# A two-layer attention and Mamba-2 kernel: the second x tile is transposed into the scan's PSUM buffers, and the second layer's start writes its decay tables with six stores

## The chip, the cores and the metric

The kernel runs on one core of a Trainium2 chip, as a single launch. The metric is the device time of one execution in microseconds. The engines are called as the profile calls them: PE (TensorE, matmuls and transposes) with its weight loads PEld, DVE (VectorE), ACT (ScalarE), POOL (GpSimd) and SP (SyncE, which here issues DMAs). "SPq" in a row of the profile is a DMA issue on SP.

## The reference

A latent stream of 1024 tokens by 1024 features goes through two layers: gated windowed attention, then a gated bidirectional Mamba-2 (SSD) mixer. Each is wrapped in an adaLN-modulated RMS norm and a gated residual. 256 context tokens supply keys and values to the attention, and initial states to the scans. The change lies wholly in the second layer:

```python
def front(h):                        # for the latents and for the context
    z, xbc, dt_raw = split(h @ w_in)
    xbc = silu(centred_depthwise_conv(xbc, conv_w, conv_b))      # 5 taps
    xs, bm, cm = split(xbc)          # xs: 8 groups x 256, bm and cm: 8 groups x 128
    dt = softplus(dt_raw + dt_bias)
...
a_cs = cumsum(dt * A, axis=chunk)    # chunks of 128 tokens, both directions
states = einsum(bm, exp(a_last - a_cs), x * dt)
h[c + 1] = exp(a_last[c]) * h[c] + states[c]
y = (cm @ bm.T * exp(a_cs[q] - a_cs[s])) @ (x * dt) + cm @ h[c] * exp(a_cs) + d_skip * x
...
y_lat = (rms_normalize_per_group(y * silu(z)) * norm_w) @ w_out
```

There are 8 groups of 4 heads with 64 columns each, 8 chunks of latents, 2 chunks of context, and everything is kept in float32. A product of matrices is made of three matmuls on a high and a low part of each operand (high by high, low by high, high by low).

## The kernel before, in words

**The groups.** The second layer works through the 8 groups one after the other. `front(g)` makes the inputs of one group: four tiles of 128 features in the order `bT` (keys), the first x tile (kind 0), the second x tile (kind 1), `cT` (queries), and then `z`. For each of the first three tiles a context part (24 matmuls of 128x256 into the PSUM buffer `psD`) comes ahead of the latent part (48 matmuls of 128x512, L1095, into a two-bank buffer `raw` of tag `pj2`); `cT` has the latent part only. `z` then takes 192 matmuls of 128x256 (L1129) into two more buffers of tag `pj2`. PSUM has two buffers `pj2` (two banks each), one `psD` and three `psX` (one bank each). The third tile's `raw` and the first buffer of `z` are therefore the same memory: between them `cT` has taken the other one.

**After the matmuls of a tile**, a queue of steps `post` works it off: an ACT bias step that empties `raw` into `acc`, four convolution taps on DVE (L1011, which still read `raw`), a tanh on ACT back into `raw` (L1018), and a DVE product (L1019) that makes the silu. For `bT` and the two x tiles, `natural` then turns the tile so that tokens lie on the partitions: PE transposes of `acc` into the used `raw` (L1058), four per step, and an ACT copy out of it (L1061) per four. The order of steps in this kernel is transposes, copy, transposes, copy. `z` may start writing when the third tile's last copy has read the buffer.

**The queue.** Each matmul that `front` issues advances the queue's clock by its cost; every POST = 0.5 us of cost pops one step. Steps posted with a delay (LATE = 3.0) wait in a second list until the clock has advanced that far. What the queue gives is the program's order; a list scheduler in the framework then simulates the whole program and reorders the instructions of every engine by readiness, so PE's order is known only from the built program.

**The scan.** While `front(g + 1)` runs, `slot` scans one chunk of group g at a time, five pieces of front work between its parts. It takes five `psX` buffers in turn: `pcb` (L1247), `po` (L1249, L1250), `S` (L1256), `yd` (L1281) and `pt` of the chunk before (L1312, two transposes into `uT`, which is stored as `uN`). `states` is a chain of 11 jobs (matmul L1198 into `psD`, POOL L1173 and L1178, DVE L1210) that makes the initial states of the next group; it starts when `st[1]` is set, that is when the second x tile is done.

**The start of the layer.** `dt_chain` makes the decays: `decay` stores the cumulated decays to DRAM (`acs_d`), `total` stores the chunk totals (`eal_d`, L951, L952) and loads them back broadcast (`eal`, L953); `rows`, at the end of the chain, loads the first two chunks' decay rows (`M` and `bw`, L1221, 256 KB each). After group 0's front, `offset` (POOL L1226), `merge` (DVE L1230, a predicated copy of `bw` into `M`) and `decays` (ACT L1236, exponentials) prepare the first chunk's decay matrix.

**The end.** The output projection (`ssd_out`, 576 matmuls on L1527 in its first part) runs beside the scan of the last group. It takes its features from the stored `uN` through a load (`oraw`, L1473), an ACT cast (L1485) and a DVE subtraction (L1482). The features of group 7 (k = 14, 15) for the first half of the tokens are first read by matmul 337 of the 576.

Of the kernel before, what the change touches and what calls it, by code (L numbers as in the profile page):

```python
# [17 lines left out]
P = 128  # L18
# [15 lines left out]
R = 4  # L34
HP = 64
# [24 lines left out]
OUT = 4 * 30 * 3 * N512  # L60
POST = 0.5
LATE = 3.0
DTPACE = 1.0
SEGS = (1.5, 2.0, 2.0, 2.2, 2.2)
_STOP = None
# [46 lines left out]
class Kernel:  # L112
# [812 lines left out]
    def dt_chain(self, keep, rows):  # L925

        nc, t, ps, p = self.nc, self.t, self.psA, self.ps_
        n = 640
        nb = n // P
        dt = self.dts  # L930
        w1, w2, w3, ea = [t(p, [P, KT // 2, 256], F32, y).rearrange("p a b -> p (a b)")[:, :n] for y in ("xn4", "sz", "sz", "xn4")]
        tot = t(self.pc, [P, 8], F32, "tot", 2)[:, :nb]
        et = t(self.pc, [P, 8], F32, "tot", 2)[:, :nb]
# [1 line left out]
        v, act = nc.vector, nc.scalar.activation  # L935

        def decay():
            for o in (0, 384):
                for y in range(4):
                    d, s = y // 2, (o // 384) * 512 + 256 * (y % 2)  # L940
                    nc.sync.dma_start(self.acs_d[32 * d : 32 * d + 32, s : s + 256], w3[32 * y : 32 * y + 32, o : o + 256])

        def total():
            v.tensor_copy(tot[:64], blocks(w3)[:64, :, P - 1])
            v.tensor_copy(tot[64:], blocks(w3)[64:, :, 0])
            act(et, tot, AF.Exp)
            for y in range(4):
                d, h = y // 2, y % 2
                row = self.eal_d[0][32 * d : 32 * d + 32]
                for o, c in ((0, 2 * h), (3, 4 + 2 * h)):  # L950
                    nc.sync.dma_start(row[:, c : c + 2], et[32 * y : 32 * y + 32, o : o + 2])  # L951
                nc.sync.dma_start(row[:, 8 + h : 9 + h], et[32 * y : 32 * y + 32, 2:3])  # L952
# [5 lines left out]
        def turn(b):  # L958
# [15 lines left out]
        steps = [  # L974
            lambda: v.scalar_tensor_tensor(w1, in0=dt, scalar=-1.0, in1=dt, op0=ALU.mult, op1=ALU.min),
            lambda: act(w1, w1, AF.Exp),
            lambda: v.tensor_scalar_add(w2, w1, 1.0),
            lambda: v.tensor_scalar_add(w3, w2, -1.0),
            lambda: (act(ea, w2, AF.Ln), v.tensor_sub(w1, w1, w3)),
            lambda: v.reciprocal(w3, w2),  # L980
            lambda: v.tensor_mul(w1, w1, w3),
            lambda: v.tensor_add(w1, w1, ea),
# [3 lines left out]
            lambda: v.tensor_tensor_scan(out=w3[:64], data0=keep[:64], data1=w1[:64], initial=0.0, op0=ALU.mult, op1=ALU.add),  # L986
            lambda: v.tensor_tensor_scan(out=w3[64:, ::-1], data0=keep[64:, ::-1], data1=w1[64:, ::-1], initial=0.0, op0=ALU.mult, op1=ALU.add),
            decay,
            total,
            lambda: v.tensor_sub(blocks(w1), tot.unsqueeze(2).broadcast_to([P, nb, P]), blocks(w3)),  # L990
            lambda: act(w1, w1, AF.Exp),
            lambda: v.tensor_sub(w2, w2, w3),
            lambda: v.tensor_mul(w1, w1, dt),
            lambda: act(ea, w3, AF.Exp),
            rows,
        ]
        return steps + [lambda b=b: turn(b) for b in (2, 0, 4, 3, 1)]

# [16 lines left out]
    def silu(self, raw, acc):  # L1015

        nc = self.nc
        return [lambda: nc.scalar.activation(raw, acc, AF.Tanh),  # L1018
                lambda: nc.vector.scalar_tensor_tensor(acc, in0=raw, scalar=1.0, in1=acc, op0=ALU.add, op1=ALU.mult)]  # L1019

    def front(self, g, st, post, first=None, dt=None):

        nc, t, a = self.nc, self.t, self.a
        ps, p, pf = self.psA, self.ps_, self.pf
# [25 lines left out]
        def wz(q):  # L1050
            return lambda: weights(a["w_z"][g, q], 4, 256)

        def natural(raw, acc, dst, o, n):
            steps = []

            def tr(lo, hi):
                for x in range(lo, hi):
                    nc.tensor.transpose(raw[:, x * P : (x + 1) * P], acc[:, x * P : (x + 1) * P], self.ident)  # L1058

            def ev(d, lo, hi):  # L1060
                nc.scalar.copy(d[:, :, o : o + P], raw[:, lo * P : hi * P].rearrange("p (c n) -> p c n", n=P))  # L1061

            for d, lo, hi in dst:
                steps.append(lambda lo=lo, hi=hi: tr(lo, hi))
                steps.append(lambda d=d, lo=lo, hi=hi: ev(d, lo, hi))
            return [(LATE, steps)]

        tiles = [(16 + g, "bT"), (2 * g, 0), (2 * g + 1, 1), (24 + g, "cT")]
        st["xn"] = [t(p, [P, 4, R * HP], F32, "xn4") for _ in range(2)] + [t(p, [P, NCC, R * HP], F32, "xn2")]
# [6 lines left out]
        for n, (x, kind) in enumerate(tiles):  # L1076
# [4 lines left out]
            if nat:  # L1081
                raw = t(ps, [P, 512], F32, "psD")[:, :CTX]
# [24 lines left out]
                    post.append(lambda: self.dt_tail(draw, post, *dt))  # L1107
            post.extend(self.taps(x, raw, acc, 0, LAT, LAT) + self.silu(raw, acc))
            if nat:
                post.extend(natural(raw, acc, [(st[nat[0]][i], 4 * i, 4 * i + 4) for i in range(2)], nat[1], 8))  # L1110

            def done(kind=kind, acc=acc):
                st[kind] = acc

            post.append((LATE, [done]) if nat else done)
        need(w)
        w0, w = w, loads[-1]()
        post.extend(w["steps"])
# [26 lines left out]
    def ssd(self, c0):  # L1145
# [16 lines left out]
        def hd(d, g):  # L1162
            return slice(32 * d + 4 * g, 32 * d + 4 * g + 4)
# [64 lines left out]
        def merge(M, bw):  # L1228

            nc.vector.copy_predicated(M, self.before.unsqueeze(1).broadcast_to([P, R, P]), bw)  # L1230
# [463 lines left out]
```

## Time and profile before

| what | before |
|---|---|
| median of 3 runs | 1809.46 us (1806.79 to 1813.08) |
| the profiled execution | 1807.02 us, span 1805.3 us |
| granted PE clock, mean | 0.993 |
| PE busy | 1739.6 us, 96% of the span |
| DVE, ACT, POOL busy | 65%, 48%, 44% |
| DMA traffic | 227.61 MB, mean 126 GB/s |

The profiled execution spends 1.7 us outside its span. In a row, "start us, us, engine line op out<-in xcount [idle before <-releaser]", the bracket is idle time of that engine ahead of the instruction and what ended it. PEclk in a table of windows is the clock granted to PE, 1.00 being full. Matmuls are pipelined: the distance from one start to the next, not the duration, is what one of them costs PE.

### The profile page before, as it was taken

How to read it: one execution, taken by the hardware profiler on the slowest of the kernel's cores; microseconds unless marked ns; L12 is line 12 of the kernel's file. 1: busy time of each engine (PE TensorE's matmuls, PEld its weight loads, DVE VectorE, ACT ScalarE, POOL GpSimd, SP SyncE). 2: the span in 40 equal slices, each digit the busy share in tenths (PEclk: the TensorE clock that was granted, in tenths of full speed). 3: DMA queues.
4: the chain of work that ended last, by engine and by line, in shares of the span. 5: the costliest groups of instructions: out<-in, count | busy, mean ns of one | idle time of the engine just before them, and what ended most of it. 6: DMA issues, size and time to landing. Idle time of an engine off the chain costs nothing.

```text
span 1805.3 us, 28983 instructions
## 1 busy us (share of the span) xinstructions
PE 1739.6 (96%) x10319; PEld 1494.7 (83%) x10319; DVE 1181.8 (65%) x2115; ACT 867.1 (48%) x1906; POOL 799.0 (44%) x1068
## 2 busy tenths in 40 slices
PE   6899999999999999999999999999999999999997
PEld 2697788888888887778888898988889898888887
DVE  4634436778877885684776858577684867766734
ACT  3612237777777774452443525344353534544522
POOL 2331127555575545103454544645454464554411
PEclk9999999999999999999999999999999999999999
DMA  9558856444455436222222323222332322656533
GB/s 334 226 144 268 283 177 149 106 100 111 111 153 130 120 102 221 73 53 73 71 77 82 92 62 98 79 71 79 81 93 62 100 73 76 174 169 170 175 101 121
DMA packets 212495, 227.61 MB, mean 126 GB/s; under 512 B 16384, under 2 KB 149632, under 8 KB 212352
## 3 DMA queue, kind: packets, MB, share of 16 engines
q1 hardware_dynamic: 178288, 207.12, 38.0%
q0 software_dynamic: 34064, 18.65, 5.8%
q8 instruction: 81, 1.33, 0.3%
q14 instruction: 62, 0.51, 0.1%
HBM read 190.88 MB, written 35.13 MB: 125 GB/s over the span
## 4 chain that ended last, share of the span: by engine, by line
PE 81%; DVE 9%; ACT 4%; DMA 3%; issue 2%; SPq 1%; POOL 1%; DVEq 0%; ACTq 0%; POOLq 0%
PE pj L1095 17%; PE pj L1129 10%; PE pj L1527 7%; PE pj L246 6%; PE pj L247 6%; PE pj L248 6%; PE psD L1085 4%; PE psX L1281 3%; PE pt L684 3%; PE psD L1198 2%; PE pv L691 2%; PE pv L690 1%; PE S L659 1%; PE S L658 1%; PE psX L1249 1%
## 5 line engine op out<-in xcount | busy, mean ns | idle before, releaser
L246 PE MATMUL pj<-uH,wh 128*128 128x512 f32 (+1 forms) x712 | 257.4, 363 | 9.0 <-ACT uH L470 6.3
L247 PE MATMUL pj<-uL,wh 128*128 128x512 f32 (+1 forms) x712 | 243.3, 342 | 0.5 <-POOL uL L707 0.4
L248 PE MATMUL pj<-uH,wl 128*128 128x512 f32 (+1 forms) x712 | 242.4, 341 | 1.4 <-POOL wl L231 1.4
L1095 PE MATMUL pj<-uH,wl 128*128 128x512 f32 x512 | 172.7, 405 | 0.0
L1095 PE MATMUL pj<-uH,wh 128*128 128x512 f32 x512 | 171.4, 405 | 1.2 <-ACT bn L1061 0.7
L1095 PE MATMUL pj<-uL,wh 128*128 128x512 f32 x512 | 169.2, 402 | 0.0
L246 PEld LDWEIGHTS pj<-uH,wh 128*128 128x128 f32 x712 | 135.6, 191 | 36.2 <-ACT uH L470 7.7
L1129 PE MATMUL pj<-wh,uH 128*128 128x256 f32 x512 | 150.3, 294 | 9.1 <-ACT xn L1061 9.1
L1173 POOL TENSOR_TENSOR xw<-xn,dtdec 128x256 f32<-128x256 f32 x144 | 92.9, 650 | 141.6 <-PE psD L1198 107.1
L1129 PE MATMUL pj<-wh,uL 128*128 128x256 f32 x512 | 152.7, 298 | 0.0
L248 PEld LDWEIGHTS pj<-uH,wl 128*128 128x128 f32 x712 | 135.0, 190 | 18.6 <-POOL wl L231 2.3
L247 PEld LDWEIGHTS pj<-uL,wh 128*128 128x128 f32 x712 | 135.8, 191 | 16.0 <-issue 3.0
L1129 PE MATMUL pj<-wl,uH 128*128 128x256 f32 x512 | 146.7, 287 | 0.0
L689 DVE TENSOR_TENSOR pl<-pt,ph 128x512 fp32r<-128x512 f32 x168 | 114.1, 688 | 47.2 <-ACT ph L688 46.2
L231 POOL TENSOR_TENSOR wl<-wr,wh 128x512 fp32r<-128x512 f32 x76 | 100.2, 1322 | 86.1 <-ACT wh L229 85.2
L663 DVE CUSTOM_DVE_ANT_0 sm<-S,mask,nsink 128x640 f32<-128x640 f32 (+2 forms) x160 | 119.2, 773 | 19.8 <-PE S L659 12.6
L665 ACT ACTIVATE sm<-sm,nm 128x640 f32<-128x640 f32 (+2 forms) x160 | 118.6, 742 | 16.6 <-DVE nm L663 15.9
L688 ACT CAST ph<-pt 128x512 fp32r<-128x512 f32 x168 | 97.5, 586 | 56.0 <-PE pt L684 52.7
L229 ACT CAST wh<-wr 128x512 fp32r<-128x512 f32 (+1 forms) x116 | 74.7, 648 | 87.7 <-PE pj L247 63.5
L1095 PEld LDWEIGHTS pj<-uH,wl 128*128 128x128 f32 x512 | 95.3, 188 | 19.2
L1095 PEld LDWEIGHTS pj<-uL,wh 128*128 128x128 f32 x512 | 95.4, 188 | 18.7
L1129 PEld LDWEIGHTS pj<-wh,uH 128*128 128x128 f32 x512 | 98.7, 193 | 13.5 <-ACT xn L1061 12.1
(339 smaller groups left out, 4810.8 us busy)
## 6 DMA issues: line engine op xcount, KB each, us to landing
wr<-w_x SPq DMA_DIRECT2D x32, 512.0 KB, 4.6
M<-acs SPq DMA_DIRECT2D x64, 256.0 KB, 4.9
bw<-acs SPq DMA_DIRECT2D x64, 256.0 KB, 5.5
wr<-w_sk SPq DMA_DIRECT2D x24, 512.0 KB, 3.8
wr<-wg SPq DMA_DIRECT2D x40, 256.0 KB, 4.5
qs<-q POOLq DMA_DIRECT2D x40, 256.0 KB, 3.9
wada<-w_ada SPq DMA_DIRECT2D x16, 512.0 KB, 7.2
wr<-wq SPq DMA_DIRECT2D x32, 256.0 KB, 3.0
```

Source lines behind the costliest of these rows:

```text
L231: (eng or nc.vector).tensor_tensor(l, raw, h, op=ALU.subtract)
L246: self.nc.tensor.matmul(ps, lh, rh, start=first and i == 0, stop=False)
L247: self.nc.tensor.matmul(ps, lh, rl, start=False, stop=False)
L248: self.last_mm = self.nc.tensor.matmul(ps, ll, rh, start=False, stop=last and i == n - 1)
L663: nc.vector.tensor_tensor_reduce(out=sm[:, :W], in0=Sv, in1=self.mask[:, m0 : m0 + W], scale=-SCALE, scalar=self.nsink[:, 4 * j + r : 4 * ...
L665: nc.scalar.activation(sm[:, :W], sm[:, :W], AF.Exp, bias=nm[:, r : r + 1], scale=-1.0, accum_out=sums[:, r : r + 1])
L688: nc.scalar.copy(ph, ptf)
L689: nc.vector.tensor_sub(pl, ptf, ph)
L1095: nc.tensor.matmul(raw[:, 512 * i : 512 * i + 512], l[:, k, :], r[i][:, k, :], start=k + y == 0, stop=k == KT - 1 and y == 2)
L1129: nc.tensor.matmul(pj[:, c], l, r[:, k, :], start=c % 2 + q + k + y == 0, stop=c % 2 == 1 and q == 1 and k == 3 and y == 2)
L1173: nc.gpsimd.tensor_tensor(xw, X(st, c).rearrange("p (r h) -> p r h", r=R), self.dtdec[:, c, hd(d, g)].unsqueeze(2).broadcast_to([P, R, HP] ...
L1527: nc.tensor.matmul(banks[x], l[:, z, sl], r, start=k == 2 * qs[0] and y == 0, stop=k == 2 * qs[-1] + 1 and y == 2)
```

## The change

**The turnings.** `natural` gets a parameter `apart`, which is set for the latent part of the second x tile. There each set of four transposes goes into a `psX` buffer of its own, and the copies read those; `raw` is no longer used after the silu product. The steps wait LAST = 6.8 instead of 3.0, and `st[1]` is set at the same delay, so that the chain of states starts later. For the other tiles both sets of transposes are one step, still into `raw`, followed by the two copies.

**The layer's start.** `decay` makes 4 stores of two halves where there were 8; `total` makes 2 where there were 12, with the columns of `eal_d` in another order that `EPOS` undoes when they are read. `rows` comes right after `decay`, ahead of `total`. On SP the order is then 4 stores of `acs`, M, bw, M, bw, 2 stores of `eald`, the load of `eal`; before it was 8 stores of `acs`, 12 of `eald`, M, bw, the load of `eal`, M, bw. The first `merge` is issued behind the last silu product in the program.

```diff
+LAST = 6.8
+EPOS = (0, 1, 5, 6, 3, 4, 8, 9, 2, 7)
...
         def decay():
-            for o in (0, 384):
-                for y in range(4):
-                    d, s = y // 2, (o // 384) * 512 + 256 * (y % 2)
-                    nc.sync.dma_start(self.acs_d[32 * d : 32 * d + 32, s : s + 256], w3[32 * y : 32 * y + 32, o : o + 256])
+            for d in range(2):
+                for o in range(2):
+                    dst = self.acs_d[32 * d : 32 * d + 32, 512 * o : 512 * o + 512].rearrange("r (h n) -> h r n", h=2)
+                    nc.sync.dma_start(dst, w3[64 * d : 64 * d + 64, 384 * o : 384 * o + 256])
...
-            for y in range(4):
-                d, h = y // 2, y % 2
-                row = self.eal_d[0][32 * d : 32 * d + 32]
-                for o, c in ((0, 2 * h), (3, 4 + 2 * h)):
-                    nc.sync.dma_start(row[:, c : c + 2], et[32 * y : 32 * y + 32, o : o + 2])
-                nc.sync.dma_start(row[:, 8 + h : 9 + h], et[32 * y : 32 * y + 32, 2:3])
+            for d in range(2):
+                nc.sync.dma_start(self.eal_d[0, 32 * d : 32 * d + 32].rearrange("r (h k) -> h r k", h=2), et[64 * d : 64 * d + 64])
             nc.sync.dma_start(self.eal, self.eal_d.broadcast_to([P, 64, NCH + NCC]))
...
             decay,
+            rows,
             total,
...
             lambda: act(ea, w3, AF.Exp),
-            rows,
...
-        return [lambda: nc.scalar.activation(raw, acc, AF.Tanh),
-                lambda: nc.vector.scalar_tensor_tensor(acc, in0=raw, scalar=1.0, in1=acc, op0=ALU.add, op1=ALU.mult)]
+        def prod():
+            self.silu_last = nc.vector.scalar_tensor_tensor(acc, in0=raw, scalar=1.0, in1=acc, op0=ALU.add, op1=ALU.mult)
+
+        return [lambda: nc.scalar.activation(raw, acc, AF.Tanh), prod]
...
-        def natural(raw, acc, dst, o, n):
+        def natural(raw, acc, dst, o, n, apart=False):
...
-            for d, lo, hi in dst:
-                steps.append(lambda lo=lo, hi=hi: tr(lo, hi))
-                steps.append(lambda d=d, lo=lo, hi=hi: ev(d, lo, hi))
-            return [(LATE, steps)]
+            def turn(d, lo, hi):
+                out, q = (t(ps, [P, 512], F32, "psX"), lo) if apart else (raw, 0)
                 for x in range(lo, hi):
-                    nc.tensor.transpose(raw[:, x * P : (x + 1) * P], acc[:, x * P : (x + 1) * P], self.ident)
+                    nc.tensor.transpose(out[:, (x - q) * P : (x - q + 1) * P], acc[:, x * P : (x + 1) * P], self.ident)
+                return lambda: nc.scalar.copy(d[:, :, o : o + P], out[:, (lo - q) * P : (hi - q) * P].rearrange("p (c n) -> p c n", n=P))
+
+            if apart:
+                for d, lo, hi in dst:
+                    out = []
+                    steps.append(lambda d=d, lo=lo, hi=hi, out=out: out.append(turn(d, lo, hi)))
+                    steps.append(lambda out=out: out[0]())
+            else:
+                out = []
+                steps.append(lambda: out.extend(turn(d, lo, hi) for d, lo, hi in dst))
+                steps += [lambda x=x: out[x]() for x in range(len(dst))]
+            return [(LAST if apart else LATE, steps)]
...
-                post.extend(natural(raw, acc, [(st[nat[0]][i], 4 * i, 4 * i + 4) for i in range(2)], nat[1], 8))
+                post.extend(natural(raw, acc, [(st[nat[0]][i], 4 * i, 4 * i + 4) for i in range(2)], nat[1], 8, kind == 1))
...
-            post.append((LATE, [done]) if nat else done)
+            post.append((LAST if kind == 1 else LATE, [done]) if nat else done)
...
-            nc.gpsimd.tensor_tensor(hn, h, self.eal[:, hd(d, g), c].unsqueeze(2).broadcast_to([P, R, HP]), op=ALU.mult)
+            nc.gpsimd.tensor_tensor(hn, h, self.eal[:, hd(d, g), EPOS[c]].unsqueeze(2).broadcast_to([P, R, HP]), op=ALU.mult)
...
         offset(0, bw[0])
-        merge(fw[0], bw.pop(0))
+        with self.tc.issue_after(self.silu_last.ins):
+            merge(fw[0], bw.pop(0))
```

The instructions of all engines up to the second layer's first projections stand as before. Three places of PE's order follow; in the rows the number after a name tells the buffer's use.

PE before, at the end of group 0's `cT` (L1095) and the start of its `z` (L1129): `pj_2194` is the second x tile's `raw`, `pj_2223` the first buffer of `z`.

```order
4190 L1095 MATMUL pj_2208_9226<-uL_2133_8671,wh_9175 128x512
4191 L1095 MATMUL pj_2208_9226<-uH_2034_8170,wl_9175 128x512
4192 L1095 MATMUL pj_2208_9226<-uH_2132_8670,wl_9175 128x512
4193 L1058 MATMUL pj_2194_9090<-ident_63,cacc_9091 128x128 x4
4194 L1198 MATMUL psD_9282<-xw_9267,bn_2163_8762 128x256
4195 L1058 MATMUL pj_2194_9090<-ident_63,cacc_9091 128x128 x4
4196 L1198 MATMUL psD_9295<-xw_9280,bn_2163_8762 128x256
4197 L1129 MATMUL pj_2223_9320<-wh_9272,uH_2034_8170 128x256
4198 L1129 MATMUL pj_2223_9320<-wl_9274,uH_2034_8170 128x256
```

PE of the changed kernel, the same place (`z` is L1135 there, the transposes L1060, a state job L1204):

```order
4189 L1101 MATMUL pj_2208_9212<-uL_2133_8671,wh_9161 128x512
4190 L1101 MATMUL pj_2208_9212<-uH_2034_8170,wl_9161 128x512
4191 L1101 MATMUL pj_2208_9212<-uH_2132_8670,wl_9161 128x512
4192 L1204 MATMUL psD_9286<-xw_9275,bn_2163_8762 128x256
4193 L1060 MATMUL psX_9256<-ident_63,cacc_9084 128x128 x4
4194 L1060 MATMUL psX_9262<-ident_63,cacc_9084 128x128 x4
4195 L1135 MATMUL pj_2219_9295<-wh_9246,uH_2034_8170 128x256
4196 L1135 MATMUL pj_2219_9295<-wl_9248,uH_2034_8170 128x256
```

The eight transposes still stand between `cT` and `z`, but they write `psX`, and one state job less stands ahead of `z`; 27 matmuls of `z` follow without a break. On DVE the silu product of this tile comes ahead of the merge, where it came behind it.

PE before, at the same place of group 1, whose front runs beside group 0's scan (`pj_2334` is `raw`, the first set of four stands 12 rows higher, at 4699):

```order
4708 L1095 MATMUL pj_2356_10160<-uH_2034_8170,wl_10087 128x512
4709 L1095 MATMUL pj_2356_10160<-uH_2132_8670,wl_10087 128x512
4710 L1247 MATMUL psX_10380<-cT_9227,bT_8798 128x128
4711 L1058 MATMUL pj_2334_10023<-ident_63,cacc_10024 128x128 x4
4712 L1249 MATMUL psX_10382<-hf_10230,cT_9227 128x256
4713 L1250 MATMUL psX_10382<-hb_2231_9361,cT_9227 128x256
4714 L1198 MATMUL psD_10217<-xw_10200,bn_2267_9619 128x256
4715 L1312 MATMUL psX_10263<-ident_63,y_2155_8749 128x128
4716 L1129 MATMUL pj_2390_10317<-wh_10211,uH_2034_8170 128x256
```

PE of the changed kernel, inside group 1's `z`, which began at row 4700 directly behind `cT`:

```order
4729 L1135 MATMUL pj_2388_10294<-wh_10187,uH_2034_8170 128x256
4730 L1060 MATMUL psX_10212<-ident_63,cacc_10012 128x128 x4
4731 L1060 MATMUL psX_10218<-ident_63,cacc_10012 128x128 x4
4732 L1135 MATMUL pj_2388_10294<-wl_10189,uH_2034_8170 128x256
4733 L1135 MATMUL pj_2388_10294<-wh_10187,uL_2035_8171 128x256
4734 L1135 MATMUL pj_2388_10294<-wh_10187,uH_2034_8170 128x256
4735 L1135 MATMUL pj_2388_10294<-wl_10189,uH_2034_8170 128x256
4736 L1135 MATMUL pj_2388_10294<-wh_10187,uL_2035_8171 128x256
4737 L1135 MATMUL pj_2388_10294<-wh_10187,uH_2034_8170 128x256
4738 L1135 MATMUL pj_2388_10294<-wl_10189,uH_2034_8170 128x256
4739 L1135 MATMUL pj_2388_10294<-wh_10187,uL_2035_8171 128x256
4740 L1204 MATMUL psD_10258<-xw_10224,bn_2269_9607 128x256
```

The transposes have moved behind 25 of the matmuls of `z`. The first to take their two `psX` buffers again are a tail's transpose at row 4746 and the next chunk's first matmul at row 4750: between the sets and these stand 12 and 15 matmuls of `z`, a state job and four matmuls of `yd`.

PE before, in the output projection, at the second tail transpose (L1312) of chunk 3 of group 7, which completes the features for the first half of the tokens:

```order
8383 L1527 MATMUL pj_3716_17715<-uH_3602_17195,wh_17806 128x512
8384 L1527 MATMUL pj_3716_17715<-uL_3603_17196,wh_17806 128x512
8385 L1312 MATMUL psX_17689<-ident_63,y_2156_8751 128x128
8386 L1527 MATMUL pj_3716_17715<-uH_3602_17195,wl_17808 128x512
8387 L1527 MATMUL pj_3717_17716<-uH_3602_17195,wh_17806 128x512
```

PE of the changed kernel, the same transpose (L1318; the output projection is L1534):

```order
8458 L1534 MATMUL pj_3733_17718<-uL_3621_17200,wh_17980 128x512
8459 L1534 MATMUL pj_3733_17718<-uH_3620_17199,wl_17982 128x512
8460 L1318 MATMUL psX_17691<-ident_63,y_2156_8751 128x128
8461 L1534 MATMUL pj_3732_17717<-uH_3620_17199,wh_18050 128x512
8462 L1534 MATMUL pj_3732_17717<-uL_3621_17200,wh_18050 128x512
```

Before, 115 matmuls of L1527 stand between this transpose and the first that reads those features (matmul 337, at row 8518). In the changed kernel it is 24 of L1534, with one each of the scan's six matmul groups among them (L1253, L1255, L1256, L1262, L1287, L1318), and the reader is at row 8491: the chain of states started later in every group, and the last scan stands about 90 matmuls further back in the projection.

More of the change, by code (lines that the diff above doesn't have):

```diff
@@ L1051, in wz @@
             return lambda: weights(a["w_z"][g, q], 4, 256)
-        def natural(raw, acc, dst, o, n):
+        def natural(raw, acc, dst, o, n, apart=False):
             steps = []
-            def tr(lo, hi):
+            def turn(d, lo, hi):
+                out, q = (t(ps, [P, 512], F32, "psX"), lo) if apart else (raw, 0)
                 for x in range(lo, hi):
-                    nc.tensor.transpose(raw[:, x * P : (x + 1) * P], acc[:, x * P : (x + 1) * P], self.ident)
-            def ev(d, lo, hi):
-                nc.scalar.copy(d[:, :, o : o + P], raw[:, lo * P : hi * P].rearrange("p (c n) -> p c n", n=P))
-            for d, lo, hi in dst:
-                steps.append(lambda lo=lo, hi=hi: tr(lo, hi))
-                steps.append(lambda d=d, lo=lo, hi=hi: ev(d, lo, hi))
-            return [(LATE, steps)]
+                    nc.tensor.transpose(out[:, (x - q) * P : (x - q + 1) * P], acc[:, x * P : (x + 1) * P], self.ident)
[10 more added lines that the diff above has]
+            return [(LAST if apart else LATE, steps)]
         tiles = [(16 + g, "bT"), (2 * g, 0), (2 * g + 1, 1), (24 + g, "cT")]
```

## The prediction

> **What bounds the kernel now.** I read the page's first part, then the groups with the longest idle time, then the waits of PE by stretch, and last the timelines of the two places that the change touches.
>
> ```profile
> PE 1739.6 (96%) x10319; PEld 1494.7 (83%) x10319; DVE 1181.8 (65%) x2115; ACT 867.1 (48%) x1906; POOL 799.0 (44%) x1068
> L1129 PE MATMUL pj<-wh,uH 128*128 128x256 f32 x512 | 150.3, 294 | 9.1 <-ACT xn L1061 9.1
> ```
>
> PE is busy for 96% of the span; no other engine is near. So the time falls only where PE stops idling or runs at a higher clock, and each microsecond PE idles is paid. The second line is the largest idle group in the second layer: `z` waits 9.1 us in all for the copies out of the third tile's `raw`. The waits of PE from 826 to 1600 us, seven groups' fronts, hold nothing else:
>
> ```profile
> PE pj L1129 <- ACT xn L1061: 9.1, 7, 1.3
> ```
>
> Seven waits, the longest 1.3: seven equal ones of 1.3. Group 1's instance, from the timelines of PE, ACT and DVE:
>
> ```profile
> 912.00 1.22 DVE L1019 SCALAR_TENSOR_TENSOR cacc<-pj,cacc 128x1024 f32<-128x1024 f32 x1
> 921.27 0.60 PE L1058 MATMUL pj<-ident,cacc 128*128 128x128 f32 x4
> 921.70 0.60 PE L1249 MATMUL psX<-hf,cT 128*128 128x256 f32 x2
> 923.00 0.27 PE L1312 MATMUL psX<-ident,y 128*128 128x128 f32 x1
> 922.45 1.20 ACT L1007 ACTIVATE cT<-pj,cb,cw 128x1024 f32<-128x1024 f32 x1
> 923.95 0.57 ACT L1061 COPY xn<-pj 128x512 f32<-128x512 f32 x1
> 924.58 0.39 PE L1129 MATMUL pj<-wh,uH 128*128 128x256 f32 x1 [1.30 <-ACT xn L1061]
> ```
>
> The second set of transposes started at 921.27, its copy only at 923.95, since ACT was at `cT`'s bias step, and `z` could start at 924.58. The last to read `raw` before the transposes is the silu product, over at 913.22, 11 us before `z` wants the memory. That product is what `z` waits for in the changed kernel.
>
> The layer's start loses more, and at two prices:
>
> ```profile
> 803.40 0.42 SPq L952 DMA_DIRECT2D eald<-tot  x1
> 804.37 1.09 SPq L1221 DMA_DIRECT2D bw<-acs  x1
> 813.97 1.04 POOL L1226 TENSOR_TENSOR bw<-bw,vd 128x512 f32<-128x512 f32 x1 [72.63 <-DMA bw<-acs]
> 815.05 0.73 DVE L1230 COPY_PREDICATED M<-before,bw 128x512 f32<-128x512 int32 x1 [5.26 <-POOL bw L1226]
> 815.92 1.22 DVE L1019 SCALAR_TENSOR_TENSOR cacc<-pj,cacc 128x1024 f32<-128x1024 f32 x1
> 810.73 1.10 ACT L1018 ACTIVATE pj<-cacc 128x1024 f32<-128x1024 f32 x1
> 813.80 0.62 PE L1095 MATMUL pj<-uL,wh 128*128 128x512 f32 x2
> 814.26 0.62 PE L1095 MATMUL pj<-uH,wl 128*128 128x512 f32 x2
> 817.19 0.66 PE L1058 MATMUL pj<-ident,cacc 128*128 128x128 f32 x4 [2.31 <-DVE cacc L1019]
> 818.14 1.22 PE L1198 MATMUL psD<-xw,bn 128*128 128x256 f32 x2 [0.29 <-POOL xw L1173]
> 819.98 1.12 PE L1058 MATMUL pj<-ident,cacc 128*128 128x128 f32 x4 [0.61 <-ACT xn L1061]
> 821.77 0.58 PE L1129 MATMUL pj<-wh,uH 128*128 128x256 f32 x1
> 825.08 0.28 PE L1129 MATMUL pj<-wh,uH 128*128 128x256 f32 x1
> 825.19 0.28 PE L1129 MATMUL pj<-wl,uH 128*128 128x256 f32 x1
> ```
>
> The `bw` load is issued behind the 12 stores of `eald`; it lands only for POOL at 813.97, the merge follows at 815.05 after 5.26 us of idle DVE, and behind it on DVE stands the third tile's product, whose tanh had ended at 811.83. PE waits 2.31, then 0.29 and 0.61. The granted clock falls with it, as the table of windows tells (PEclk is the number ahead of the last two):
>
> ```profile
> 818.00:820.00 2.00, 1.25 (x3) 0.53 (x3) 1.62 (x2) 2.00 (x4) 1.22 (x3) 0.54 0.56 146
> 820.00:822.00 2.00, 2.00 (x7) 1.46 (x8) 1.97 (x2) 0.78 (x2) 0.84 (x2) 0.50 0.90 272
> 824.00:826.00 2.00, 2.00 (x15) 2.00 (x14) 1.09 (x1) 0.81 (x1) 0.00 (x0) 0.75 0.00 0
> ```
>
> So about 7 us, 818 to 825, ran at half clock, behind the idle time of 814.88 to 817.19 and what followed it.
>
> **Part by part: the layer's start.** With the product ahead of the merge on DVE, it waits for its tanh alone and is over at about 811.83 + 1.22 = 813.1, before `cT`'s matmuls end. These are two per 0.46 us, so the one after the last would start at 814.72. From there PE has one state job (0.43) and eight transposes (0.43 per four, 921.27 to 921.70) before `z`, without a wait: `z` starts at 814.72 + 0.43 + 0.86 = 816.0 for 821.77. One state job of 0.43 is done later, so 5.3 us are gained. The half-clock stretch goes with its idle time: from 821.77 to 825.08 PE issued 15 matmuls of `z` at 0.22 us, 3.3 us in all, where 0.12 each (825.08 to 825.19) would make 1.8. That is 1.5 more, together **−6.8 us**.
>
> Whether the first state job finds its operands is the open end. It needs POOL L1173, which stands behind `offset` (813.97 + 1.04). With `rows` ahead of `total` and with four stores for eight the `bw` load is issued at least 12 × 0.42 = 5 us earlier, so `offset` is over by about 810, if the transfer is as long as before. If it lands where it did, the job starts at about 815.01 + 0.6 = 815.6 and the gain is 0.9 smaller. Were the merge still ahead, all of it would be lost; it isn't, by DVE's order. The load of `eal` comes out at about its old time, and its first reader is later than the first job: nothing. The rows give a store 0.42 us of issue on SP, and only these follow one another. The Trainium skill's page "DMA: Bandwidth & Descriptors" (Anatomy of one DMA) puts a fixed 2 us on every DMA, mostly completion latency; were that paid in turn, 12 stores fewer ahead of `bw` would move it 24 us and not 5, which the rows do not bear out, and `z` would start no earlier for it, as `cT` binds by then.
>
> **Part by part: the seven fronts.** `z` starts behind `cT` with the `raw` of a product long over: **−9.1 us**. The transposes are the same eight and cost PE what they did. They need two `psX` buffers more per group. Between them and the next users of those two buffers PE has 12 and 15 matmuls of `z` (0.12 each), a state job (0.43) and the four of `yd` (0.39): 2.3 and 2.6 us. In that time two copies of 0.57 must run, 1.2 us with a little handing over, if ACT is free. Inside `z` it is:
>
> ```profile
> 925.41 0.51 ACT L1300 ACTIVATE y<-y,ss 128x256 f32<-128x256 f32 x1 [0.34 <-POOL ss L1296]
> 929.78 1.03 ACT L1018 ACTIVATE pj<-cT 128x1024 f32<-128x1024 f32 x1 [3.85 <-DVE cT L1011]
> ```
>
> If a copy has to stand 2.1 us behind other ACT work, as it did at 923.95 (921.87 to 923.95), each is 0.4 us late: 0 to +2.8 in all, and I take **+0.6**, near the end that the 3.85 us of idle ACT supports.
>
> The one-step turnings of `bT` and the first x tile remain in `raw`. They give `raw` up one step later or earlier by less than 0.5 us, and no wait of those tiles shows in the seven fronts: nothing, up to +1 if a group lacks the slack.
>
> **Part by part: the end.** The chain of states starts later in each group, so the last scan runs further into the output projection. Chunk 3 of group 7 is complete 24 projection matmuls before matmul 337 reads it (115 before). Its path is a `uT` copy, a store, a load, a cast and a subtraction:
>
> ```profile
> L1313 ACT ACTIVATE uT<-psX,nw 128x128 f32<-128x128 f32 x128 | 46.5, 363 | 114.4 <-PE psX L1312 114.3
> uN<-uT SPq DMA_DIRECT2D x64, 128.0 KB, 3.2
> oraw<-uN SPq DMA_DIRECT2D x32, 256.0 KB, 4.0
> L1473 SPq DMA_DIRECT2D oraw<-uN x18: 319/320/430, 1657.8 to 1708.7; - x18
> L1485 ACT CAST uH<-oraw x18: 606/617/624, 1661.6 to 1711.6; 128x512 fp32r<-128x512 f32 x18
> L1482 DVE TENSOR_TENSOR uL<-oraw,uH x18: 677/688/1786, 1662.3 to 1712.2; 128x512 fp32r<-128x512 f32 x18
> ```
>
> That is 0.36 + 3.2 + 4.0 + 0.62 + 0.69 and two issues of some 0.32, 9.5 us. PE covers 24 × 0.23 = 5.5 and about 1.9 of scan matmuls, 7.4. So a new wait of **+2.1 us**; 0 if the transfers are quick, +5.7 if each takes half as long again, and 3.5 more if the idle time halves the clock as at 818.
>
> **The sum.** −6.8 − 9.1 + 0.6 + 2.1 = −13.2. The profiled execution (1807.02, of which 1805.3 is span) would come to 1793.8. It lies 2.4 us under the median of 1809.46; from the median it is **1796.3**.
>
> **The rivals.** (A) *The seven stalls only move.* `z` starts, and PE stops 1.3 us per group later, at a `psX` buffer or at a state chain that is now late. For it: three buffers, five users per chunk and two more. Against it: the idle ACT above. Then −13.2 + 9.1 = −4.1, 1805.4.
>
> (B) *Start and end give little.* The loads of `M` and `bw` contend and the gain at the start is halved (+3.4), and the features come at the upper bound with the clock down (+7.1): −2.7, 1806.8. For it: nothing in the trace has ever shown this short a distance. Against: both must come together.
>
> The clock around group 1's wait of 1.30, from the same kind of table:
>
> ```profile
> 922.00:926.00 4.00, 2.69 (x19) 2.25 (x18) 3.96 (x8) 3.58 (x8) 3.16 (x5) 1.00 0.60 139
> 926.00:930.00 4.00, 4.00 (x34) 3.95 (x33) 3.96 (x5) 0.22 (x1) 3.57 (x5) 1.00 0.41 137
> ```
>
> (C) *Slower, through the clock.* PE idles at a new place for as long as at 817.19, 2.3 us, in each of the seven groups: a `psX` transpose waiting on a copy queued behind exponentials, casts and bias steps, with PE's own order stopped behind it. Then each costs 2.3 + 3.5 (7 us at half clock) = 5.8, 40.6 in all: −13.2 + 40.6 = +27.4, 1836.9. It decides from about 2.3 us of idle per group; at 1.3 the clock holds, 1.00 in both rows. For it: 2.1 us behind other work is what the copy at 923.95 waited. Against: that wait would have to reach PE whole, and it has 2.3 us of cover. The Trainium skill's page "TensorE: Matmul & The Clock Gate" (A second HAM failure mode: psum-queue depth-cycling) speaks for C: it tells of a kernel whose small idles between PSUM banks made the clock swing. Here seven idles of 1.3 us at a bank cost nothing beyond themselves, so the trace does not bear it out below 2.3.
>
> (D) *The change doesn't do what it says*, and `z` still waits on the third tile's buffer: nothing in the order supports it, 1809.5 less the start, 1802.7.
>
> **How the numbers follow.** A measurement of this kernel can tell about 0.3%, 5.4 us, from no change. The forecast gets 0.73, A 0.09, B 0.06, C 0.10, D 0.02. Faster by over 0.3% is the forecast and D, 0.75; within it are A and B, 0.15; slower is C, 0.10. The forecast alone reaches from 1791 (no wait at the end, none at `psX`, −15.9, and 2.4 for the place of the profiled run against the median) to 1803 (the end's upper bound and `psX`'s). The range takes in A and B: 1790 to 1807.
>
> **What would show it.** In the changed profile `z`'s line (L1135) has no wait for ACT in the seven fronts and starts at about 816.0 in group 0, with the clock at 1.00 through 816 to 826. The projection (L1534) shows one wait of some 2 us for the features' cast, or none. I am wrong if waits for `psX` users on PE sum to over 3 us, if the 800 to 850 stretch shows a clock under 0.9, or if the whole gain is less than 5.

## The result, and the profile after

| | before | changed |
|---|---|---|
| median of 12 runs | 1811.18 us (1806.3 to 1813.51) | 1812.01 us (1804.75 to 1815.87) |
| ratio of the runs | | 1.0006, 95% interval 0.9995 to 1.0016 |
| the profiled execution | 1807.02 us, clock 0.993 | 1804.75 us, clock 0.993 |
| second layer in that execution | 1057.5 us | 1057.0 us |

No change that a measurement can tell; 13 us less had been forecast. The profiled execution of the changed kernel is the fastest of its 12 and reached the second layer 2.0 us earlier than that of before, with the same instructions up to there. So times inside the second layer are counted below from its first matmul on L1085 (L1091 changed), at 747.86 us before and 745.87 after.

What the change aimed at came. The start, from the timelines of PE and DVE of the changed kernel:

```profile
809.87 1.23 DVE L1018 SCALAR_TENSOR_TENSOR cacc<-pj,cacc 128x1024 f32<-128x1024 f32 x1 [0.71 <-ACT pj L1020]
812.91 1.04 PE L1060 MATMUL psX<-ident,cacc 128*128 128x128 f32 x8
813.70 0.36 PE L1135 MATMUL pj<-wh,uH 128*128 128x256 f32 x1
```

The product waits for its tanh alone, nothing waits at the transposes, and `z` starts 67.8 us into the layer, for 73.9 before. The table of windows, before and after, for the ten microseconds in which `z` of group 0 begins before (in the changed kernel it began at 813.70):

```profile
816.00:826.00 10.00, 7.90 (x35) 6.40 (x36) 7.79 (x8) 5.59 (x11) 3.81 (x6) 0.66 0.54 157
```

```profile
816.00:826.00 10.00, 10.00 (x81) 9.84 (x81) 6.69 (x8) 2.68 (x6) 3.40 (x5) 1.00 0.18 62
```

PE ran at a granted 0.66 and with 2.1 us idle; now it is full at 1.00. The seven waits at `z` are gone too. In their place stand these, all of PE's waits from 826 to 1760 us of the changed kernel:

```profile
PE pj L1534 <- DVE uL L1540: 3.0, 1, 3.0
PE pj L1101 <- DVE wl L1039: 1.7, 3, 0.7
PE psD L1204 <- DVE hb L1216: 1.6, 1, 1.6
PE psD L1204 <- ACT hx L1208: 1.4, 1, 1.4
PE pj L1534 <- DVE uH L1540: 1.3, 1, 1.3
PE psX L1253 <- DVE hf L1263: 1.0, 1, 1.0
PE psX L1262 <- POOL xw L1179: 0.8, 1, 0.8
PE psX L1262 <- ACT uT L1319: 0.6, 1, 0.6
PE pj L1534 <- DVE wl L1470: 0.4, 1, 0.4
PE psX L1318 <- DVE hf L1263: 0.4, 1, 0.4
PE pj L1534 <- DVE sz L1146: 0.2, 1, 0.2
PE psX L1287 <- DVE M L1257: 0.2, 1, 0.2
```

They make 12.6 us for 9.1, and none comes before 1392 us. Two thirds lie in the last fronts and at the head of the output projection, the other 4.3 (L1540) further inside the projection. There PE needs a `pj` bank whose result DVE has not yet taken; the DVE instruction that takes it is called the gate below. The windows of before and after for the same 20 us (busy time of PE, PEld, DVE, ACT and POOL, then PEclk):

```profile
1680.00:1700.00 20.00, 19.97 (x95) 16.23 (x94) 10.03 (x15) 9.47 (x18) 6.29 (x6) 1.00 0.56 186
```

```profile
1680.00:1700.00 20.00, 15.79 (x72) 12.73 (x71) 20.00 (x26) 13.90 (x29) 13.45 (x10) 0.91 0.52 159
1684.00:1692.00 8.00, 6.63 (x22) 5.26 (x23) 8.00 (x9) 5.62 (x13) 4.95 (x3) 0.79 0.42 137
```

DVE is busy for all of the 20 us, for 10 before, PE loses 4.2, and behind the wait of 3.0 the clock falls to 0.79 over 8 us, 1.7 us more. What fills DVE in these 20 us is mostly one line, the subtraction that makes the low part of the projection's features, before and after (count, busy us, mean ns):

```profile
L1482 DVE TENSOR_TENSOR uL<-oraw,uH 128x512 fp32r<-128x512 f32 x2 | 1.3, 678 | 0.0
L1489 DVE TENSOR_TENSOR uL<-oraw,uH 128x512 fp32r<-128x512 f32 x8 | 9.4, 1215 | 0.0
```

The scan itself has some 3.7 us of DVE there, for 1.5 before; the gates and the splitting of weights hardly change. The eight subtractions belong to the second half of the tokens. In the order of DVE they stand behind those of the features of group 7 (k = 14 and 15) for the first half, and these need the scan of the last group: they come 928.0 and 930.2 us into the layer, for 914.4 and 916.8 before. That scan runs beside the projection and comes later than before. Its lateness shows in one row of DVE per chunk, the product with `z`. Here are the last chunk of group 6 and the first of group 7, before and after:

```profile
1586.89 0.83 DVE L1293 TENSOR_TENSOR y<-y,sz 128x256 f32<-128x256 f32 x1
1608.79 0.79 DVE L1293 TENSOR_TENSOR y<-y,sz 128x256 f32<-128x256 f32 x1
```

```profile
1577.57 0.79 DVE L1299 TENSOR_TENSOR y<-y,sz 128x256 f32<-128x256 f32 x1
1620.67 0.79 DVE L1299 TENSOR_TENSOR y<-y,sz 128x256 f32<-128x256 f32 x1
```

The step between groups, 21.9 us before, is 43.1 after. Over the groups it was 28.6 six times and then 21.9; after the change it is 27.1, 29.7, 30.6, 31.1, 35.2, 32.4, 43.1. The scan falls back from group to group, and the last chunk of all ends 26 us later in the layer (962.1 for 936.2) although the projection begins 12 us earlier (829.5 for 841.6).

The sum of the second layer: −9.1 for the seven waits, −5.6 for the start (6.1 less a state job of 0.43 done later), −1.5 for the clock there, +12.6 for the new waits, +1.7 for the new half-clock stretch, −1.9 together; −0.4 is measured. Of the missing 1.5, 0.9 lie behind the last matmul of the projection's first part (from its start to the end of the span 62.2 us, for 61.3); the rest is not accounted for. The other 11 runs of the changed kernel had mean clocks of 0.989 to 0.992 for the profiled one's 0.993; their places are not known.

### The profile page after: what moved, and what is told of

Its sections match the earlier page's. It is cut to its first block, busy times and chain, and to the rows that moved or that the text cites. A ratio compares the mean times of both kernels' runs of the same rounds, so it can differ in the third digit from the quotient of the medians.

```text
span 1802.9 us, 28981 instructions
## 1 busy us (share of the span) xinstructions
PE 1736.8 (96%) x10319; PEld 1494.5 (83%) x10319; DVE 1183.5 (66%) x2115; ACT 873.8 (48%) x1906; POOL 808.8 (45%) x1068
## 4 chain that ended last, share of the span: by engine, by line
PE 79%; DVE 10%; DMA 4%; issue 3%; ACT 3%; POOL 1%; SPq 0%; DVEq 0%; ACTq 0%; POOLq 0%
PE pj L1101 18%; PE pj L1135 10%; PE pj L248 6%; PE pj L249 6%; PE pj L250 6%; PE pj L1534 6%; PE psD L1091 3%; PE pt L686 3%; PE psX L1287 3%; PE pv L693 2%; PE psD L1204 2%; PE pv L692 2%; PE S L661 1%; PE S L660 1%; PE psX L1255 1%
## 5 line engine op out<-in xcount | busy, mean ns | idle before, releaser
L1101 PE MATMUL pj<-uH,wl 128*128 128x512 f32 x512 | 168.1, 401 | 1.7 <-DVE wl L1039 1.7
L248 PEld LDWEIGHTS pj<-uH,wh 128*128 128x128 f32 x712 | 135.6, 191 | 33.5 <-issue 6.1
L1135 PE MATMUL pj<-wh,uL 128*128 128x256 f32 x512 | 151.4, 296 | 0.0
L1135 PE MATMUL pj<-wl,uH 128*128 128x256 f32 x512 | 151.4, 296 | 0.0
L1135 PE MATMUL pj<-wh,uH 128*128 128x256 f32 x512 | 150.9, 295 | 0.0
L667 ACT ACTIVATE sm<-sm,nm 128x640 f32<-128x640 f32 (+2 forms) x160 | 118.6, 742 | 16.5 <-DVE nm L665 15.9
L1101 PEld LDWEIGHTS pj<-uH,wh 128*128 128x128 f32 x512 | 95.1, 188 | 21.4 <-ACT bn L1061 1.4
```

The costliest lines, as they stand in the source:

```text
L248: self.nc.tensor.matmul(ps, lh, rh, start=first and i == 0, stop=False)
L667: nc.scalar.activation(sm[:, :W], sm[:, :W], AF.Exp, bias=nm[:, r : r + 1], scale=-1.0, accum_out=sums[:, r : r + 1])
L1101: nc.tensor.matmul(raw[:, 512 * i : 512 * i + 512], l[:, k, :], r[i][:, k, :], start=k + y == 0, stop=k == KT - 1 and y == 2)
L1135: nc.tensor.matmul(pj[:, c], l, r[:, k, :], start=c % 2 + q + k + y == 0, stop=c % 2 == 1 and q == 1 and k == 3 and y == 2)
```

## The experiments

Theory 1 was that the chain of states starts too late (LAST = 6.8), theory 2 that the shared `psX` buffers or the one-step turnings make PE wait by themselves, theory 3 that the scan needs its 105.8 us per group and falls behind when a front gets shorter. All runs were timed against before. Beside each ratio stands what PE's planned order of that kernel says of the scan: the place of each group's last state job (the matmul of the chain `states`), counted in front work since that group's front began. A matmul of 256 columns is 1, one of 512 is 2, and a whole front is 648.

| kernel | second x tile in `psX`, LAST | other tiles | last state job of groups 1 to 7 | second layer, us | ratio (95%) |
|---|---|---|---|---|---|
| before | no | two steps | 718 six times, 714 | 1057.5 | |
| changed | 6.8 | one step | 722 728 760 774 834 840 910 | 1057.0 | 1.0006 (0.9995 to 1.0016) |
| start only | no | two steps | as before | 1053.2 | 0.9976 (0.9964 to 0.9987) |
| turnings only | 6.8 | one step | as changed | 1066.0 | 1.0044 (1.0028 to 1.0059) |
| one step | no | one step | 760 758 772 800 840 816 782 | 1070.8 | 1.0064 (1.0043 to 1.0085) |
| 3.0 | 3.0 | one step | 760 790 840 840 840 840 734 | 1070.4 | 1.0078 (1.0064 to 1.0092) |
| 0.5, one step | 0.5 | one step | 764 774 800 764 806 762 768 | 1052.5 | 0.9980 (0.9968 to 0.9993) |
| 4.0, one step | 4.0 | one step | 746 six times, 792 | 1046.6 | 0.9938 (0.9922 to 0.9953) |
| 8.0, one step | 8.0 | one step | 730 734 730 734 730 734 748 | 1043.3 | 0.9923 (0.9907 to 0.9939) |
| 6.8, two steps | 6.8 | two steps | 734 760 766 840 840 840 904 | 1061.2 | 1.0031 (1.0017 to 1.0046) |
| 4.0, two steps | 4.0 | two steps | 730 six times, 768 | 1044.4 | 0.9923 (0.9904 to 0.9943) |
| 0.5, two steps | 0.5 | two steps | 726 736, 738 four times, 740 | 1042.4 | 0.9912 (0.9894 to 0.9929) |
| filled | 6.8 | one step | 716 six times, 714 | 1048.2 | 0.9952 (0.9935 to 0.9969) |
| group 0 apart | 6.8, group 0 | two steps | 716 686 625 630 630 630 643 | 1055.3 | 0.9989 (0.9974 to 1.0004) |

**Start only.** The edits of `dt_chain`, `silu` and `EPOS`, with `natural` as before.

> Only the layer's start is changed (six stores, rows ahead of total, the merge behind the product); the turnings are as before. Both theories expect the same: z of group 0 starts some 6 us earlier and no half-clock stretch at 818, so 6.5 to 8 us faster than before (ratio 0.9958 to 0.9964), the seven waits of 1.3 us for the copies stay, and the output projection shows no new wait. If instead the start's gain is lost further on, the ratio is 1.000.

4 us and not the 6.5 to 8 expected: the transposes still go into `raw`, and the second set waits for the copy of the first.

```profile
818.35 0.66 PE L1059 MATMUL pj<-ident,cacc 128*128 128x128 f32 x4 [1.38 <-ACT xn L1062]
```

The half-clock stretch is gone, and the gain stays to the end. So the start is good by itself.

**Turnings only.** The edit of `natural`, with the start as before.

> Only the turnings are changed; the start is as before. Theory 1 (the chain of states starts later, so the last scan reaches 80 to 110 matmuls further into the projection, where DVE is full and PE waits for its gates): the seven waits are gone (-9), the waits of groups 5 to 7 and of the projection are there as in the changed kernel (+12 and a half-clock stretch): 3 to 9 us slower than before, ratio 1.002 to 1.005. Theory 2 (sharing the three psX buffers makes PE wait) expects the same here.

8 us slower, as expected, with the changed kernel's late waits nearly one for one, the two on DVE's gates at 2.7 each, and two half-clock stretches of 3.4 us, at the head of the projection and at the second of these gates. With the old start PE also waits 5.3 us in one piece for POOL, at group 0's first state job, where before lost 3.2 in three waits. The turnings, meant to win 9.1 us, cost 8, and the start takes 7 of these off again in the changed kernel.

**LAST = 3.0.**

```diff
-LAST = 6.8
+LAST = 3.0
```

> The changed kernel with LAST = 3.0 for 6.8: the turnings still go to psX, but they and the start of the chain of states come as early as before. By PE's order the last scan's tails stand where they stood before (120 to 360 of the 576 matmuls, for 201 to 470). Theory 1: start and the seven waits are gained and nothing is given back, 12 to 16 us faster than before, ratio 0.991 to 0.9935. Theory 2: the psX waits stay and the gain is 0 to 6, ratio 0.9967 to 1.000.

Theory 1 falls in this form: with the chain of states free to start as early as before, the kernel is 14 us slower than before. Its tails stand where they stood, but its state jobs slide to 840, and five of the last group's are crowded at one place at the head of the projection, where PE waits longest for the scan (the two longest rows of its waits from 1575 to 1745 us):

```profile
PE psX L1287 <- DVE M L1257: 3.4, 1, 3.4
PE psD L1204 <- DVE hb L1216: 2.0, 3, 0.8
```

Behind the 3.4 the clock is halved for 13.7 us, some 6.8 us lost beside the 7.8 of all waits there. The table of windows:

```profile
1600.00:1614.00 14.00, 11.36 (x30) 7.67 (x31) 7.04 (x18) 3.72 (x10) 9.62 (x15) 0.52 0.41 92
```

The place of the last tails alone, which I had read in the order, says too little; the state jobs do.

**One step, nothing apart.**

```diff
-... nat[1], 8, kind == 1))
+... nat[1], 8))
-            post.append((LAST if kind == 1 else LATE, [done]) if nat else done)
+            post.append((LATE, [done]) if nat else done)
```

> The changed kernel with the second x tile turned in raw like the others, both sets in one step, at 3.0. By PE's order the tails stand between (145 to 423). Theory 1: the start is gained (-7), the seven waits stay or grow, and part of the projection's waits comes (+2 to +6): ratio 0.997 to 1.000. Theory 2: no psX sharing, no new waits: 7 us faster, ratio 0.996.

1.0064, where start only gave 0.9976: turning both sets in one step costs some 16 us without any use of `psX`. Theory 2's half on `psX` falls, and the expected gain with it. The longest waits are of state jobs:

```profile
PE psD L1204 <- DVE hb L1216: 5.9, 4, 2.6
PE psD L1204 <- ACT hx L1208: 4.1, 2, 2.4
```

**Filled.** The changed kernel with work added where the seven waits were:

```diff
             for q in range(2):
                 ww = (w0, w)[q]
                 need(ww)
+                if i == q == 0 and g:
+                    for _ in range(11):
+                        nc.tensor.matmul(pj[:, 0], uH[0][:, 0, :P], ww["h"][:, 0, :], start=True, stop=True)
```

> The changed kernel with 11 matmuls of 128x256 added ahead of each z of groups 1 to 7 (they repeat z's first product and are overwritten by it): 11 x 0.12 = 1.3 us of PE work where the seven waits were, 9.1 us in all. Theory 3 (the scan's own chain needs some 105.8 us per group; a front that takes 104.5 leaves the scan behind, group by group): by PE's order the state jobs and the tails of the last scan stand where they stood before (tails 119 to 360), so the late waits and the projection's waits go, and with 9.1 us more work the kernel is 5 to 8 us faster than the changed one and than before, ratio to before 0.9956 to 0.997. Theory 2 (psX sharing or the one-step turnings make PE wait by themselves): the waits stay and the work is added, 8 to 10 us slower than the changed kernel, ratio 1.004 to 1.006.

77 useless matmuls, 9.2 us at 0.12 each, make the changed kernel some 10 us faster. The group of the added line:

```profile
L1132 PE MATMUL pj<-wh,uH 128*128 128x256 f32 x77 | 12.5, 292 | 0.0
```

And all of PE's waits from 826 to 1760 us:

```profile
PE pj L248 <- ACT xs L1433: 0.2, 1, 0.2
PE pj L1537 <- DVE sz L1149: 0.2, 1, 0.2
```

So it isn't `psX`, nor one step, nor 6.8 by itself, since all three are still there. Thirteen of the changed kernel's fourteen waits went when the order stopped sliding. Its second layer is 8.8 us shorter; the waits and the half-clock stretch less the added work make 4.7 of these, and the other 4.1 are not accounted for.

**Two steps, LAST = 0.5.** The buffers are still chosen by `apart`, only the order of the steps isn't:

```diff
-LAST = 6.8
+LAST = 0.5
...
-            if apart:
+            if True:
                 for d, lo, hi in dst:
```

> The changed kernel with LAST = 0.5 for 6.8, and the other tiles turned in two steps as before. By PE's order the state jobs are steady from group 3 on (491 to 738 of 648 front units) and the tails of the last scan stand at 128 to 360. If the order's drift is what costs (theory 3 in its weak form), the seven waits and the start are gained: ratio 0.991 to 0.994. If the scan's chain really needs 105.8 us per group on the chip (strong form), PE waits for it elsewhere, about 1.3 us per group: 0.995 to 0.998. Theory 2: 1.000 to 1.005.

The fastest, 16 us under before. All of PE's waits from 826 to 1750 us:

```profile
PE pj L1534 <- DVE wl L1470: 1.4, 1, 1.4
PE psD L1204 <- DVE hb L1216: 0.7, 1, 0.7
PE pj L248 <- ACT xs L1430: 0.2, 1, 0.2
PE psX L1287 <- DVE M L1257: 0.2, 1, 0.2
```

From group 3 on to group 6 the scan goes along at 104.1 us per group, so the strong form of theory 3 falls: the chip can do without the 1.3 us. What needs them, or another order, is the plan.

**Two steps, LAST = 6.8.** The same with LAST = 6.8.

> The changed kernel with the other tiles turned in two steps as before; the second x tile in psX at 6.8. By PE's order the tails stand as far back as in the changed kernel (201 to 470). Theory 3: the same late waits, ratio 0.998 to 1.003. If the one-step turnings of the other tiles are the cause: 0.991 to 0.994.

1.0031 for 0.9912, from one constant. The one-step turnings are not the cause either, where the delay makes the order slide.

**LAST = 8.0, 4.0 and 0.5.** The changed kernel with another constant, and the one with two steps at 4.0. These were chosen because the planned order is steady at 8.0 and 4.0, and not at 0.5 with one step.

> The changed kernel with LAST = 8.0 for 6.8 and nothing else. By PE's order the state jobs of groups 1 to 6 end at 730 to 734 of 648 front units in every group (722 rising to 840 in the changed kernel), and the last scan's tails stand at 127 to 384 (201 to 470). Drift theory (what costs is that the scan falls further behind from group to group in the planned order, whatever the delay): no waits in groups 1 to 6, ratio to before 0.991 to 0.9935. Delay theory (the later the turnings and the chain of states, the worse): as slow as the changed kernel or slower, 1.000 to 1.005.

> The changed kernel with LAST = 4.0. By PE's order steady again (last state job at 746 in groups 2 to 6; tails 146 to 384). Drift theory: ratio 0.991 to 0.994. Delay theory: between the kernels with 3.0 (1.0078) and 6.8 (1.0006), 1.000 to 1.008.

> The second x tile in psX with LAST = 4.0, the other tiles in two steps as before. By PE's order steady (last state job at 730; tails 136 to 384). Drift theory: like the kernel with two steps and 0.5 (0.9912), 0.990 to 0.993. One-step turnings as a cost of their own would show as a difference of over 0.002 to the kernel with one step and 4.0.

> The changed kernel with LAST = 0.5, the other tiles in one step. By PE's order not steady (last state job at 764, 774, 800, 764, 806, 762 in groups 1 to 6), though the last scan's tails come out early (136 to 384). Drift theory: in between, waits in groups 3 to 6 but few in the projection, 0.994 to 1.001. Delay theory: the fastest with one step, 0.991 to 0.993.

A longer delay than the change's is 15 us faster than it. The delay theory is out, and these four times follow the steadiness of the order: 0.9923, 0.9938, 0.9923 where the last state job keeps its place, 0.9980 where it wanders.

But a steady order is not enough; over all these kernels the waits go with the place itself. With 3.0 the last state job stands still at 840 in groups 3 to 6, and PE waits 2.2 to 2.9 us in each of the four fronts that follow. Where it stands between 716 and 760 and the second x tile goes to `psX` in every group, no next front has more than 0.9 us of waits; at 800 and beyond every next front waits, 0.8 to 6.6 us; in between it is mixed. One step against two at 4.0 differs by 0.0015, within the intervals. PE's waits at 8.0, from 826 to 1760 us:

```profile
PE pj L1101 <- ACT bn L1061: 1.8, 3, 0.6
PE pj L1534 <- ACT wh L1466: 1.3, 1, 1.3
PE pj L248 <- ACT xs L1430: 0.2, 1, 0.2
PE psX L1255 <- DVE y L1298: 0.2, 1, 0.2
PE psX L1253 <- DVE hf L1263: 0.2, 1, 0.2
```

The 1.8 us are at `bT`'s copies out of `raw`, the lack of slack that the prediction had bounded at 1.

**Group 0 apart.** Two steps, and `kind == 1 and g == 0` in the two places where `kind == 1` stood.

> The changed start, and the turnings into psX in group 0 alone; all other tiles as before. Start gained as in the changed kernel, 6 to 8 us, the seven waits stay, and by PE's order the last scan stands a little earlier than before (tails 83 to 360): ratio 0.9955 to 0.997 under every theory. If the ratio is above 0.998, the start's gain is lost in another way.

A miss: 0.9989. Here the order slides the other way and then stands, state jobs at 625 to 630, and groups 4 to 7 wait about 1.7 us each, mostly for POOL and ACT, where they had waited 1.3, at 107.0 us per group for 105.8: too early a place costs as well. Those waits explain 0.4 of the 1.2 us; the rest was not found.

## Why the prediction was wrong

**What held.** The product was over at 811.1, 65.2 us into the layer, as worked out (813.1 on before's time); `z` started at 815.7 on that time, for 816.0 forecast; the clock stayed at 1.00; the wait for ACT at `z` went in all seven groups; no wait came between the two uses of a `psX` buffer in groups 1 to 4. The `bw` load was issued 3.5 us earlier in the layer and not 5, but `offset` was over at 808.2 on before's time, ahead of the 810 worked out, so this didn't bind.

The section of the Trainium skill that the prediction names for 2 us per DMA ("DMA: Bandwidth & Descriptors", Anatomy of one DMA) gives that figure for the gpsimd path. The stores here are issued on SP, and in the profile of before those of `acs` landed a median of 1.6 us after issue and those of `eald` 1.4.

**The step that failed** is the price of "the chain of states starts later in each group, so the last scan runs further into the output projection". I had the shift from the order, about 90 matmuls, and put on it only the path of the features of one chunk: +2.1. PE never waited for those features. What came instead is 8.3 us of waits in the last fronts and at the head of the projection, 4.3 at the gates of a DVE that was full, mostly with the subtractions of the next features, and 1.7 of half clock: 14.3 for 2.1. The prediction had the subtraction as 0.69 us of one path, not as work that stands ahead of the gates on DVE. A scan that ends 90 matmuls later after 7 groups is one that loses ground in each, and I treated its lateness as one delay at the end. Reading the place of the last state job in every group (722 to 910, where before it is 718 six times and then 714) would have shown it.

**A second step** was unspoken: seven equal waits of 1.3 us were taken for seven independent losses. That they can be taken out without loss is shown (0.9912 and 0.9923), and that the changed kernel gains, and its planned order becomes periodic again, when work is put in their place is shown too (filled). So the 15.9 us of its two gains are there to be had (the second layer is 15.1 shorter with two steps and 0.5), and were lost in the order that this edit got.

**The rivals.** A came nearest in what happens, with "a state chain that is now late" as one of its two forms, but at 1805.4 and in every group alike; B was nearest in the number, 1806.8, but the start gave its full gain and PE never waited for the features. Neither reached the 1812.01. For A 0.09 was too little: the trace of before can't show a plan's stability, and the changed order, which could, was read at three places only. C did not happen: no group idled 2.3 us in one piece, and the projection's wait of 3.0 cost 1.7 us of clock. But its point of decision, 2.3 us, is too high: the last section shows half clock behind shorter waits. The Trainium skill tells of a kernel in which frequent small idles between matmul groups made the clock swing ("TensorE: Matmul & The Clock Gate", A second HAM failure mode: psum-queue depth-cycling). These runs bear out that short idles can do it, not that they must be frequent: here it struck single waits in single executions, and the seven waits of 1.3 not at all in the profile of before.

**Open.** Why a plan slides at 3.0 and 6.8 and stands at 0.5 (with two steps), 4.0 and 8.0 was not studied. That the planned order is what costs is shown: one constant, which changes nothing but the order, moves the ratio from 0.9923 (8.0) to 1.0078 (3.0). That the place of the state jobs causes the waits, and is not only a sign of it, and how each late wait follows, was read from orders and traces and not tested.

## What to carry to other kernels

In a software pipeline whose order is planned ahead, compare the whole period from group to group, not the place that was edited: count where one late instruction of each group stands, and look for a number that grows or that settles far from where it stood. A small regular wait may be what holds the pattern; take it out only with a look at the pattern after, and try a few values of any delay that decides it, since the time need not follow the delay in one direction. When the work that was deferred meets the program's end, look at what else the late engine has to do there.

## What the runs showed of the hardware

The clock can halve behind a wait well under 2.3 us. In the kernel with one step and 4.0, PE waited 0.51 and 1.16 us at group 0's `bT`, with 1.1 us of transposes between the two; the table of windows has the clock at 0.57 behind them:

```profile
784.00:788.00 4.00, 2.67 (x15) 1.82 (x14) 4.00 (x5) 2.84 (x4) 0.00 (x0) 1.00 0.00 0
788.00:792.00 4.00, 3.65 (x9) 2.89 (x10) 4.00 (x6) 0.29 (x1) 0.00 (x0) 0.57 0.34 131
```

In the kernel with two steps and 4.0, one wait of 1.8 at the head of the projection did it:

```profile
1574.00:1578.00 4.00, 2.23 (x11) 1.54 (x10) 3.20 (x5) 4.00 (x7) 2.05 (x4) 1.00 0.95 283
1578.00:1582.00 4.00, 4.00 (x12) 3.13 (x11) 3.80 (x6) 1.41 (x3) 1.01 (x1) 0.57 0.73 222
```

The changed kernel's profile has the same two waits of 0.51 and 1.16 at `bT`, with the clock at 1.00 behind them, so the same idle time halves it in one execution and not in another. And the first layer, the same instructions in all these kernels, ended at 745.3 to 754.6 us in the profiled executions: single executions compare two kernels only to some 10 us, while the length of the second layer followed the ratios far better.
